# Linear attention on one core: a clear of 128x2080 elements in sixteen instructions, and one load in five DMAs

## Chip, core and metric

The kernel runs on one core of one Trainium2 chip. The metric is the device time of one execution in microseconds (us), taken here as the median of four runs. One further execution was recorded by the hardware profiler, and all rows below come from it.

## What is computed

The inputs Q, K and V have 8 batches, 12 heads, 512 rows and 64 columns, in float32.

```python
Q_feat = np.maximum(0, Q) + 1
K_feat = np.maximum(0, K) + 1
KV = np.einsum('bhkd,bhkv->bhdv', K_feat, V)
K_sum = np.sum(K_feat, axis=2)
numerator = np.einsum('bhqd,bhdv->bhqv', Q_feat, KV)
denominator = np.einsum('bhqd,bhd->bhq', Q_feat, K_sum)
return (numerator / (denominator[:, :, :, None] + 1e-10)).astype(np.float32)
```

For every head a 64x64 matrix KV and a 64-vector K_sum are made from K and V, and each row of Q is multiplied with them and divided. Everything is read once and the result is written once: the page counts 37.75 MB read and 12.58 MB written.

## The kernel before

The 96 heads are worked through in twelve groups of eight heads (g from 0 to 11), and two groups make a pair s. `load("k", ...)` and `load("v", ...)` bring K and V of a group or of a pair into SBUF (the on-chip memory of 128 partitions) and turn float32 into bf16 on the way; `load_q(s)` brings Q of a pair. All these loads are issued by GpSimd (POOL), as are the stores of groups 0 to 9. Only the first K (`load_first_k`) and the last four stores are issued by SyncE (SP).

For each group, `k_features` (VectorE, DVE) makes K_feat; `v_blocks` copies V into a block layout `v_all` in four copies of 32 partitions, of which DVE makes b = 0, 1 and 2 and ScalarE (ACT) makes b = 3 (partitions 96 to 127); `keys_values` (TensorE, PE) accumulates KV and K_sum in `kva_ps`, which ACT casts into the weights `kva_all` (lines 179 and 180). `q_features`, `transposes` and `out_matmuls` make the numerator and denominator, `norms` (DVE) divides, and `store` writes.

`kva_all` holds four slots of four blocks b, each 128 partitions by 130 elements of bf16. Parts of each block must be zero and stay so; the kernel clears them once at its start, on POOL. Slot g % 4 is written by ACT for group g.

The order of instructions on each engine is that of the program text (`manual_schedule`). POOL works in this order: the clear of `zero`, the loads of V of group 0, Q of pair 0, K of group 1, V of group 1; then the identity matrix (`make_identity`, two instructions, needed by the first transposes); then the clear of `kva_all` (line 257); then `load_pair(1)`, which is K, V and Q of pair 1. After that come `load_pair(2)` and the later ones, each K and V load waiting until the compute engines have read the buffer that it overwrites, with two buffers in turn, and the stores.

The loads that POOL issues all go through one software DMA queue, which the page calls q0. In the program as built, DMAs issued by POOL signal their completion on eight semaphores in turn. A DMA that gets a semaphore for the second time is preceded by a wait on POOL until the DMA that used it before, eight DMAs back, has landed; where the same wait has been made already, it isn't made again.

Of the kernel before, what the change touches and what calls it, by code (L numbers as in the profile page):

```python
# [19 lines left out]
def kernel(  # L20
# [19 lines left out]
    nc = tc.nc  # L40

    B, H, S, D = Q.shape
    P = 128
# [36 lines left out]
    kva_all = const.tile([P, NV, 4, 2, D1], BF16, name="kva_all")  # L80
    kva_diag = [kva_all[:, i] for i in range(NV)]

    drams = dict(k=k_dram, v=v_dram)
    raw = {}
    bufs = {}
# [6 lines left out]
    def load_first_k():  # L92
        k_raw = head_pool.tile([P, 2, C2, D], FP32, name="k_first")
        nc.sync.dma_start(out=k_raw, in_=k_dram[:, 0:4:2])
        raw["k", 0] = k_raw

    def load(x, groups):
        s = groups[0] // 2
        if groups[0] % 2 == 0 or (x, s) not in bufs:
            bufs[x, s] = in_pool.tile([P, 4, C2, D], BF16, name=f"{x}_raw")  # L100
        if len(groups) == 2:
            ms = slice(0, 4)
            of = slice(4 * s, 4 * s + 4)
        else:
            ms = slice(groups[0] % 2, 4, 2)
            of = slice(4 * s + groups[0] % 2, 4 * s + 4, 2)
        nc.gpsimd.dma_start(out=bufs[x, s][:, ms], in_=drams[x][:, of])  # L107
        for g in groups:
            raw[x, g] = bufs[x, s][:, g % 2 : 4 : 2]

    def load_q(s):
        t = in_pool.tile([P, 2, C4, D], BF16, name="q_raw")
        nc.gpsimd.dma_start(out=t, in_=q_eights[:, 2 * s : 2 * s + 2])  # L113
        rows = t.rearrange("p n (r c) d -> p n r c d", c=C)
        for e in range(2):
            raw["q", 2 * s + e] = rows[:, :, :, 4 * e : 4 * e + 4]

    def load_pair(s):
        load("k", (2 * s, 2 * s + 1))
        load("v", (2 * s, 2 * s + 1))  # L120
        load_q(s)

    def store(g):
        s = g // 2
        o_to = o_dram[:, 2 * NP * s : 2 * NP * s + 2 * NP]
        if g < NG - 2:
            nc.gpsimd.dma_start(out=o_to[:, g % 2 : 2 * NP : 2], in_=outs[s][:, g % 2 : 2 * NP : 2])  # L127
            return
        for h in range(2):
            nc.sync.dma_start(  # L130
                out=o_to[:, 2 * h + g % 2 : 2 * NP : NP], in_=outs[s][:, 2 * h + g % 2 : 2 * NP : NP]
            )
# [6 lines left out]
    def k_features(g):  # L139
        k_raw = raw.pop(("k", g))  # L140
        kf = kf_pool.tile([P, C2, 2, D], BF16, name="kf")
        for n in range(2):
            feature(kf[:, :, n], k_raw[:, n])
        kfs[g] = kf

    def v_blocks(g):
        v_raw = raw.pop(("v", g))
        for b in range(4):
            ps = slice(32 * b, 32 * b + 32)
            if b == 3:  # L150
                nc.scalar.copy(out=v_blk[g % 2][ps, b], in_=v_raw[ps])  # L151
            else:
                nc.vector.tensor_copy(out=v_blk[g % 2][ps, b], in_=v_raw[ps])  # L153

    def q_features(g):
        q_raw = raw.pop(("q", g))
        qf = qf_pool.tile([P, R, C // 2, 2, D], BF16, name="qf")
        for n in range(2):
            feature(qf[:, :, :, n], q_raw[:, n])
        qfs[g] = qf  # L160

    def keys_values(g):
        kf = kfs.pop(g)
        sb = g % 2
        vb = v_all[:, 4 * sb : 4 * sb + 5]
        kva_ps = psum_kva.tile([P, 5, D], FP32, name="kva_ps")
        for c in range(C2):
            for n in range(2):
                nc.tensor.matmul(  # L169
                    kva_ps[64 * n : 64 * n + 64],  # L170
                    lhsT=kf[:, c, n, :],
                    rhs=vb[:, :, n, c, :],
                    start=(c == 0),
                    stop=(c == C2 - 1),
                )
        kva = kva_diag[g % NV]
        for n in range(2):
            ps = slice(64 * n, 64 * n + 64)
            nc.scalar.copy(out=kva[ps, :, n, 0:D], in_=kva_ps[ps, sb : sb + 4, :])  # L179
            nc.scalar.copy(out=kva[ps, :, n, D], in_=kva_ps[ps, 4 - 4 * sb, 0:4])  # L180

    def transposes(g):
        qf = qfs.pop(g)
        if g % 2 == 0:
            qts[g // 2] = mid_pool.tile([P, C, P, R], BF16, name="qt")
        for half in range(2):
            qt_ps = psum_qt.tile([P, 2, R, P], BF16, name="qt_ps")
            for c in range(2):
                for r in range(R):
                    nc.tensor.transpose(qt_ps[:, c, r], qf[:, r, 2 * half + c, :, :], identity)  # L190
            copy = nc.vector.tensor_copy if half and g == NG - 2 else nc.scalar.copy
            lo = g % 2 * 4 + 2 * half
            copy(out=qts[g // 2][:, lo : lo + 2], in_=qt_ps.rearrange("p c r q -> p c q r"))  # L193

    def out_matmuls(g, h):
        qt = qts[g // 2]
        kva = kva_diag[(g // 2 * 2 + h) % NV]
        ops = [psum.tile([P, 2, BANK], FP32, tag="ps", name="o_ps") for _ in range(2)]
        for c in range(C):
            for j in range(2):  # L200
                b = 2 * (g % 2) + j
                q = 16 * (4 * h + b)
                nc.tensor.matmul(  # L203
                    ops[c // 4][64 * j : 64 * j + 64, c // 2 % 2, (c % 2) * W : (c % 2) * W + W],
                    lhsT=qt[:, c, q : q + 16, :],
                    rhs=kva[:, b],
                    start=True,
                    stop=True,
                )
        cells_of[g, h] = ops  # L210
# [19 lines left out]
    def output(g):  # L230
        for h in range(2):
            out_matmuls(g, h)
            norms(g, h)

    def clear(first, split, end):
        t = v_all.rearrange("p b m c d -> p (b m c d)").bitcast(FP32)
        w = t.shape[1] // 9
        nc.vector.memset(t[:, first * w : split * w], 0.0)  # L238
        nc.scalar.copy(  # L239
            out=t[:, split * w : end * w], in_=zero.to_broadcast([P, (end - split) * w])  # L240
        )

    with tc.manual_schedule():
        nc.gpsimd.memset(zero, 0.0)
        load_first_k()
        load("v", (0,))
        load_q(0)
        load("k", (1,))
        load("v", (1,))
        nc.vector.memset(ones, 0.0)  # L250
        for b in range(4):
            nc.vector.memset(ones[32 * b : 32 * b + 32, b : b + 1], 1.0)  # L252
        clear(0, 3, 5)
        e = v_all[:, 4, :, :, 0:4].rearrange("p n c j -> p (n c) j")
        nc.vector.tensor_copy(out=e, in_=ones[:, None, :].to_broadcast([P, 2 * C2, 4]))
        make_identity(nc, identity)
        nc.gpsimd.memset(kva_all, 0.0)  # L257
        load_pair(1)
        clear(5, 7, 9)
        last = NG - 1  # L260
        for g in range(last - 1):
            if g % 2:
                transposes(g - 1)
            k_features(g)
            v_blocks(g)
            if g >= 2:
                output(g - 2)
            if g % 2:
                transposes(g)
            else:  # L270
                q_features(g)
                q_features(g + 1)
            keys_values(g)
            if g % 2 and g // 2 + 2 < NG // 2:
                load_pair(g // 2 + 2)
            if g >= LAG:
                store(g - LAG)
        k_features(last - 1)
        output(last - 3)
        out_matmuls(last - 2, 0)  # L280
        v_blocks(last - 1)
        k_features(last)
        v_blocks(last)
        keys_values(last - 1)
        store(last - 1 - LAG)
        q_features(last - 1)
        q_features(last)
        keys_values(last)
        norms(last - 2, 0)
        out_matmuls(last - 2, 1)  # L290
        norms(last - 2, 1)
        transposes(last - 1)
        transposes(last)
        output(last - 1)
        output(last)
        for g in range(last - LAG, NG):
            store(g)
# [30 lines left out]
```

## Time and profile before

| | us |
|---|---|
| runs | 126.93, 127.02, 127.17, 126.81 |
| median of the runs | 126.97 |
| the profiled execution's own time | 126.93 |
| its span in the profile | 124.8 |
| DVE, PE, ACT, POOL busy | 89.3, 67.0, 60.5, 25.4 |

The span runs from the first recorded instruction to the last event; 2.13 us of the profiled execution's own time lie outside it. In the lines of a timeline the first number is the start in us from the span's start, the second the busy time, then follow engine, line, operation, the tiles written and read with partitions x elements, and the count; a bracket at the end tells how long the engine had been idle and what ended that. The page's slices are 40 equal parts of the span, 3.12 us each; a digit is a busy share in tenths. For loads that cast, GB/s counts the bf16 bytes that are written, half of the bytes read.

### The profile page before, as it was taken

To read this page: it belongs to the slowest core of one execution; us is meant where nothing else is said; L and a number is where in the kernel's file an instruction comes from. 1 tells how busy PE (TensorE), PEld (TensorE's weight loads), DVE (VectorE), ACT (ScalarE), POOL (GpSimd) and SP (SyncE) were. 2 spreads that over 40 slices of the span, in tenths; PEclk is the share of its full clock that TensorE was granted. 3 is DMA by queue.
4 is the path that set the end of the run, shared out by engine and by line. 5 is a ranking of instruction groups with operands and counts; after the bars stand their busy time and mean duration, and the time that the engine had idled before them with its cause. 6 is when DMAs were issued, how large, how long until landed. Compare 5 with 4: busy or idle time off the path is not lost.

```text
span 124.8 us, 2326 instructions
## 1 busy us (share of the span) xinstructions
PE 67.0 (54%) x960; PEld 51.1 (41%) x960; DVE 89.3 (72%) x189; ACT 60.5 (48%) x86; POOL 25.4 (20%) x37
## 2 busy tenths in 40 slices
PE   0006955300694847729777490069696359965510
PEld 0004634300473736518565380056485246753300
DVE  4893444206999899998899940799958799387940
ACT  7832199306019972776447771600994291373000
POOL 6990023100011540215302150302020200020000
PEclk9999999955589999995999999756999955899855
DMA  3999999999999999999999999999999999999993
GB/s 100 327 219 208 211 195 209 211 213 216 207 212 213 216 214 209 211 213 219 230 410 320 211 211 216 216 341 393 227 211 217 217 263 415 418 415 416 408 394 127
DMA packets 11818, 32.12 MB, mean 257 GB/s; under 512 B 544, under 2 KB 544, under 8 KB 11808
## 3 DMA queue, kind: packets, MB, share of 16 engines
q0 software_dynamic: 10448, 28.84, 97.3%
q1 hardware_dynamic: 1360, 3.15, 6.7%
q8 instruction: 7, 0.11, 0.3%
q14 instruction: 3, 0.02, 0.0%
HBM read 37.75 MB, written 12.58 MB: 403 GB/s over the span
## 4 chain that ended last, share of the span: by engine, by line
DMA 52%; DVE 19%; PE 13%; ACT 7%; issue 3%; POOL 2%; POOLq 0%; DVEq 0%
DMA v_raw<-in_V_dram 52%; PE kva_ps L169 10%; DVE o_sb L221 8%; DVE v_all L153 7%; ACT v_all L151 3%; ACT qt L193 2%; PE qt_ps L190 2%; DVE recip L220 2%; DVE qf L135 1%; DVE qt L193 1%; ACT kva_all L179 1%; PE o_ps L203 1%; POOL v_raw L107 1%; POOL k_raw L107 1%; DVE kf L135 1%
## 5 line engine op out<-in xcount | busy, mean ns | idle before, releaser
L169 PE MATMUL kva_ps<-v_all,kf 128*64 128x320 bf16 x384 | 36.5, 358 | 15.2 <-DVE v_all L153 14.7
L203 PE MATMUL o_ps<-kva_all,qt 128*64 128x130 bf16 x384 | 19.4, 235 | 34.2 <-DVE recip L220 20.3
L169 PEld LDWEIGHTS <-kf 128*64 128x64 bf16 x384 | 26.1, 133 | 23.2 <-DVE v_all L153 15.0
L153 DVE COPY v_all<-v_raw 32x2048 bf16<-32x2048 bf16 x36 | 26.0, 723 | 13.1 <-DMA v_raw<-in_V_dram 12.7
L221 DVE TENSOR_TENSOR o_sb<-o_ps,recip 128x512 f32<-128x512 f32 x48 | 33.2, 692 | 1.7
L151 ACT COPY v_all<-v_raw 32x2048 bf16<-32x2048 bf16 x12 | 22.6, 1893 | 15.3 <-DMA v_raw<-in_V_dram 15.1
L203 PEld LDWEIGHTS <-qt 128*64 128x64 bf16 x384 | 13.5, 115 | 39.4 <-issue 18.9
L179 ACT CAST kva_all<-kva_ps 64x256 bf16<-64x256 f32 x24 | 8.9, 371 | 33.1 <-PE kva_ps L169 33.0
L193 ACT COPY qt<-qt_ps 128x1024 bf16<-128x1024 bf16 x23 | 22.3, 1015 | 3.9 <-PE qt_ps L190 3.5
L127 POOL DMA_DIRECT2D out_dram<-o_sb x10 | 8.5, 855 | 35.3 <-DVE o_sb L221 28.3
L190 PE MATMUL qt_ps<-identity,qf 128*128 128x128 bf16 x192 | 14.0, 228 | 2.5 <-ACT qt L193 2.0
L135 DVE TENSOR_SCALAR kf<-k_raw 128x1024 bf16<-128x1024 bf16 x22 | 8.6, 431 | 7.3 <-DMA k_raw<-in_K_dram 7.3
L190 PEld LDWEIGHTS <-qf 128*128 128x128 bf16 x192 | 11.7, 102 | 5.0 <-issue 3.7
L220 DVE RECIPROCAL recip<-o_ps 128x8 f32<-128x8 f32 x48 | 9.6, 201 | 3.7 <-PE o_ps L203 3.2
L107 POOL DMA_DIRECT2D k_raw<-in_K_dram x6 | 4.8, 801 | 36.0 <-DVE kf L135 36.0
L135 DVE TENSOR_SCALAR qf<-q_raw 128x1024 bf16<-128x1024 bf16 x24 | 8.8, 431 | 2.7 <-DMA q_raw<-in_Q_dram 2.7
L107 POOL DMA_DIRECT2D v_raw<-in_V_dram x7 | 5.4, 766 | 14.5 <-ACT v_all L151 10.7
L238 DVE MEMSET v_all<- 128x3072 f32 (+1 forms) x2 | 4.4, 2192 | 1.1 <-DVE ones L252 0.7
L113 POOL DMA_DIRECT2D q_raw<-in_Q_dram x6 | 4.3, 710 | 0.0
L180 ACT CAST kva_all<-kva_ps 64x4 bf16<-64x4 f32 x24 | 4.1, 169 | 0.0
L239 ACT COPY v_all<-zero 128x2048 f32<-128x2048 f32 x2 | 3.7, 1894 | 0.0
L257 POOL MEMSET kva_all<- 128x2080 bf16 x1 | 1.8, 1825 | 0.0
(13 smaller groups left out, 5.4 us busy)
## 6 DMA issues: line engine op xcount, KB each, us to landing
out_dram<-o_sb POOLq DMA_DIRECT2D x10, 1024.0 KB, 25.6
q_raw<-in_Q_dram POOLq DMA_DIRECT2D x6, 1024.0 KB, 26.4
k_raw<-in_K_dram POOLq DMA_DIRECT2D x5, 1024.0 KB, 21.8
v_raw<-in_V_dram POOLq DMA_DIRECT2D x5, 1024.0 KB, 23.0
out_dram<-o_sb SPq DMA_DIRECT2D x4, 512.0 KB, 4.6
k_first<-in_K_dram SPq DMA_DIRECT2D x1, 1024.0 KB, 4.9
v_raw<-in_V_dram POOLq DMA_DIRECT2D x2, 512.0 KB, 10.6
k_raw<-in_K_dram POOLq DMA_DIRECT2D x1, 512.0 KB, 12.7
```

What stands on the lines that cost most here:

```text
L107: nc.gpsimd.dma_start(out=bufs[x, s][:, ms], in_=drams[x][:, of])
L127: nc.gpsimd.dma_start(out=o_to[:, g % 2 : 2 * NP : 2], in_=outs[s][:, g % 2 : 2 * NP : 2])
L135: nc.vector.tensor_scalar(out=dst, in0=src, scalar1=1.0, scalar2=1.0, op0=ALU.add, op1=ALU.max)
L151: nc.scalar.copy(out=v_blk[g % 2][ps, b], in_=v_raw[ps])
L153: nc.vector.tensor_copy(out=v_blk[g % 2][ps, b], in_=v_raw[ps])
L169: nc.tensor.matmul(kva_ps[64 * n : 64 * n + 64], lhsT=kf[:, c, n, :], rhs=vb[:, :, n, c, :], start=(c == 0), stop=(c == C2 - 1),)
L179: nc.scalar.copy(out=kva[ps, :, n, 0:D], in_=kva_ps[ps, sb : sb + 4, :])
L190: nc.tensor.transpose(qt_ps[:, c, r], qf[:, r, 2 * half + c, :, :], identity)
L193: copy(out=qts[g // 2][:, lo : lo + 2], in_=qt_ps.rearrange("p c r q -> p c q r"))
L203: nc.tensor.matmul(ops[c // 4][64 * j : 64 * j + 64, c // 2 % 2, (c % 2) * W : (c % 2) * W + W], lhsT=qt[:, c, q : q + 16, :], rhs=kva[:, ...
L220: nc.vector.reciprocal(out=recip, in_=cells[:, :, :, :, D:D1])
L221: nc.vector.tensor_tensor(out=o_sb[:, 2 * h + g % 2 : 2 * NP : NP, 4 * i : 4 * i + 4].rearrange("p n (b c) d -> p b c n d", b=2), in0=cell ...
```

## The change

The load of V of group 1 becomes five DMAs, of partitions 0 to 111, 112 to 121, 122 and 123, 124 and 125, and 126 and 127. Together they move the same bytes to the same places. The clear of `kva_all` becomes sixteen instructions, one for each of the four blocks of the four slots, 130 elements on each partition, instead of one of 2080.

```diff
@@ load
-        nc.gpsimd.dma_start(out=bufs[x, s][:, ms], in_=drams[x][:, of])
+        parts = (0, 112, 122, 124, 126, P) if (x, groups) == ("v", (1,)) else (0, P)
+        for lo, hi in zip(parts, parts[1:]):
+            nc.gpsimd.dma_start(out=bufs[x, s][lo:hi, ms], in_=drams[x][lo:hi, of])
@@ start of the schedule
-        nc.gpsimd.memset(kva_all, 0.0)
+        for t in kva_diag:
+            for b in range(4):
+                nc.gpsimd.memset(t[:, b], 0.0)
```

In the program as built, the four further DMAs take four further completion semaphores, so the turn comes round earlier: K of pair 1 now waits on POOL for V of group 0 to land, V of pair 1 for Q of pair 0, Q of pair 1 for K of group 1, and K of pair 2 for the 112-partition part of V of group 1. Before, these four waited for no semaphore of that kind, or, for K of pair 2, for K of group 1. V of pair 2 waits for the other four parts. From Q of pair 2 on, a DMA waits for the same DMAs as before. The b = 0, 1 and 2 copies of V of group 1 wait for the 112-partition part alone, and ACT's copy b = 3 waits for all five parts. The orders of instructions on PE, DVE, ACT and SP are as they were.

## Prediction

> **What bounds the kernel.** I read the slices of the page first, then its table of DMA queues, then the chain of waits.
>
> ```profile
> DMA  3999999999999999999999999999999999999993
> GB/s 100 327 219 208 211 195 209 211 213 216 207 212 213 216 214 209 211 213 219 230 410 320 211 211 216 216 341 393 227 211 217 217 263 415 418 415 416 408 394 127
> q0 software_dynamic: 10448, 28.84, 97.3%
> DMA 52%; DVE 19%; PE 13%; ACT 7%; issue 3%; POOL 2%; POOLq 0%; DVEq 0%
> ```
>
> The sixteen DMA engines are busy in every slice but the first and the last, and one queue, q0, makes up 97.3% of their span. Two rates stand out: about 212 GB/s where casting loads run (bf16 bytes) and about 415 GB/s where stores run. The 36.7 MB that the casting loads read are 18.35 MB written, 86.6 us at 212 GB/s; the 12.58 MB of stores are 30.3 us at 415 GB/s; the first K, 1.05 MB, takes about 3 us. The sum is 120 of the 124.8 us. So the transfers bound the kernel from about 2 us on until the end: a microsecond in which the queue stands dry or an engine of it has more to carry is paid once in full, and a delay elsewhere is free while the queue stays filled. The chain says the same more roughly, with 52% on waits for V. Now the place of the change, on POOL:
>
> ```profile
> 3.56 0.74 POOL L107 DMA_DIRECT2D v_raw<-in_V_dram  x1
> 4.27 0.25 POOL masks.py:197 MEMSET identity<- 128x128 bf16 x1
> 4.60 0.29 POOL masks.py:199 TENSOR_SCALAR_AFFINE_SELECT identity<-identity 128x128 bf16<-128x128 bf16 x1
> 4.83 1.82 POOL L257 MEMSET kva_all<- 128x2080 bf16 x1
> 6.61 1.03 POOL L107 DMA_DIRECT2D k_raw<-in_K_dram  x1
> 7.63 0.80 POOL L107 DMA_DIRECT2D v_raw<-in_V_dram  x1
> 8.42 0.71 POOL L113 DMA_DIRECT2D q_raw<-in_Q_dram  x1
> 16.64 0.77 POOL L107 DMA_DIRECT2D k_raw<-in_K_dram  x1 [7.51 <-DVE kf L135]
> 20.74 0.74 POOL L107 DMA_DIRECT2D v_raw<-in_V_dram  x1 [3.34 <-DVE v_all L153]
> ```
>
> The first line is the load that is split and the fourth the clear that is split; lines five to seven are pair 1, and the last two are K and V of pair 2. POOL stands idle for 7.51 us before K of pair 2. The consumers tell when the transfers land:
>
> ```profile
> 8.20 2.16 DVE L153 COPY v_all<-v_raw 32x2048 bf16<-32x2048 bf16 x3
> 13.04 1.44 DVE L135 TENSOR_SCALAR qf<-q_raw 128x1024 bf16<-128x1024 bf16 x4 [2.69 <-DMA q_raw<-in_Q_dram]
> 15.58 0.76 DVE L135 TENSOR_SCALAR kf<-k_raw 128x1024 bf16<-128x1024 bf16 x2 [1.11 <-DMA k_raw<-in_K_dram]
> 18.11 2.09 DVE L153 COPY v_all<-v_raw 32x2048 bf16<-32x2048 bf16 x3 [1.77 <-DMA v_raw<-in_V_dram]
> 23.39 0.76 DVE L135 TENSOR_SCALAR kf<-k_raw 128x1024 bf16<-128x1024 bf16 x2 [3.19 <-DMA k_raw<-in_K_dram]
> 29.09 2.11 DVE L153 COPY v_all<-v_raw 32x2048 bf16<-32x2048 bf16 x3 [4.93 <-DMA v_raw<-in_V_dram]
> ```
>
> V of group 0, Q of pair 0 (twice the bytes), K of group 1, V of group 1, K and V of pair 1 (twice the bytes) land at 8.2, 13.0, 15.6, 18.1, 23.4 and 29.1 us: in the order of issue, one behind the other, 2.5 us for each MiB read, with no gap. What was issued at 6.61 us lands at 23.4, because the queue is full.
>
> **POOL's time.** Splitting the load adds four DMA issues. An issue occupies POOL for 0.71 to 0.74 us when nothing disturbs it, for 128 partitions of one or two MiB alike, so I take 4 x 0.73 = 2.9 us; for far fewer partitions it could be less, down to 0. The identity then starts at 4.27 + 2.9 = 7.2 us, and is done by 7.8. Its first reader, the transposes of group 0, starts at 14.82 us, so 7 us of cover stay. For the clear I have two rows: 1.82 us for 2080 elements, 0.875 ns each, and 0.25 us for the identity's 128, hence about 0.14 us fixed. Sixteen of 130 elements are 16 x (0.14 + 0.114) = 4.0 us if they don't overlap, and 1.8 us, as before, if their fixed parts overlap entirely. POOL comes to the loads of pair 1 between 9.6 us and 11.8 us, instead of at 6.61; I take 11.8, since single small instructions are what the 0.25 us row shows. The first clear is needed by ACT's cast of `kva_ps` for group 0, at 14.98 us, so 3 us cover all sixteen and more the first four.
>
> **The waits on POOL.** K of pair 1 waits for V of group 0 (8.2 us), already past. V of pair 1 waits for Q of pair 0, and goes at about 13.1 us instead of 7.63. Q of pair 1 waits for K of group 1, and goes at 15.6 us instead of 8.42. Behind these stand only K of pair 2 (16.64 us, now also waiting for the 112 partitions, which land about 17.8 us) and V of pair 2 (20.74 us, already later than its new waits). When must a load be issued so that the queue doesn't run dry? Its predecessor's landing minus the time from issue to data. The latter is bounded by two DMAs: V of group 0 was issued at 1.29 and landed 6.8 us later with 2.5 us of data of its own, so at most 4.3 us; the last stores from SP landed at the least 4.0 us after issue with 1.26 us of data each, so at most 2.7. I take 4.3 us, the dearer and the one from the same queue. K of pair 1 must go by 18.1 - 4.3 = 13.8 us and goes at 11.8, 2 us of cover. V of pair 1 must go by 23.4 - 4.3 = 19.1 and goes at 13.1; Q of pair 1 by 24.8 and goes at 15.6; K of pair 2, behind three more MiB-sized steps, has over 10 us. So all of POOL's delay is hidden, and nothing else gets late next: the cost is 0.
>
> **The consumers of V of group 1.** The DVE copies wait for 112 of 128 partitions, 7/8 of 2.5 us, and may start 0.3 us sooner, while ACT's copy at 18.09 us waits for five semaphores, 4 more at some 0.03 us each (the short "issue" pieces of the chain). Behind ACT's copy stand its copies of `qt` and the next `kva_all` casts, and PE's second `keys_values` waits for it: 0.1 us later at most. The kernel's next need of this is V of pair 2, issued at 20.74 with queue work until 34 us. Nothing reaches the end: 0.
>
> **The queue's own work.** Bytes are unchanged. Each DMA ends with a signal, so there are four more in the queue. One DMA of 2 MiB (13.04 - 8.20 = 4.84 us) costs no more than two of 1 MiB (2.54 and 2.53 us): a DMA's own cost in the filled queue is 5.07 - 4.84 = 0.23 us at most and about nothing at least, where the landings' scatter is as big. For tiny DMAs I take the low part, 0.025 us each: +0.1 us, with bounds of 0 and 0.9.
>
> [...]
>
> The open item is which of the sixteen engines carry the small DMAs. All DMAs of before have 128 partitions, eight to an engine if shared evenly, so one partition is 2.5 / 8 = 0.31 us. The 112 make seven each, and 16 partitions remain. Shared one to an engine, as 10 + 2 + 2 + 2 allows, they cost nothing; begun each time at the same engine, two engines carry 7 + 1 + 3 = 11 partitions, 0.92 us more than before, and six carry seven, 0.31 us less. I take even sharing, which the even load of before is nearest to, and keep both ends.
>
> [...]
>
> **Sum.** 126.93 (the profiled execution's own time) + 0 (POOL) + 0 (consumers) + 0.1 (queue) = 127.03; the median of the runs is 0.04 above that execution, so 127.07, rounded to 127.05.
>
> **Rivals.** The first ends slower: the small DMAs fall on the same engines. As the queue is never dry, the excess on those two is not given back. It decides where the loaded engines are also among the last to finish; it costs 0.92 us then, 127.95, and nothing if they had 0.92 us to spare. For it: nothing in the rows says where a DMA begins. Against it: nothing as well.
>
> The second, also slower: POOL is late. DVE's features and copies run nearly without pause from 6.7 to 10.4 us, and K of pair 1's issue of 1.03 us, against 0.75 elsewhere, shows that POOL suffers beside them. If the clears stood still until 10.4 us, K of pair 1 would go at 14.4, 0.6 us past 13.8: 127.6. Against it: the next two issues, 0.80 and 0.71 us, lie beside the same DVE copies and are not stretched.
>
> The third ends faster: the engines that get one partition less are those that finish last; the end moves by 0.31 us, to 126.65.
>
> **Numbers.** The forecast has 0.45, the first rival 0.22, the second 0.10, the third 0.23. A measurement of this kernel can tell about 0.2%, 0.25 us, from no change. Of the forecast 0.40 lies inside that, the rest above it; a little of the first rival, with engines that have room, lies inside too. Faster 0.23, same 0.42, slower 0.35. The range goes from the third rival, 126.6, to nearly the whole of the first, 127.8.
>
> **What would show it.** Right: POOL's clears end by 12 us, the three loads of pair 1 are issued at about 11.8, 13.1 and 15.6 us, V and K of pair 1 land within 0.2 us of 29.1 and 23.4, the DMA row has 9 in every slice from the second, and V of the last pair is copied at 98.9 us as before. A K of pair 1 that lands more than 0.3 us late with a dip in the DMA row means POOL was late; one that lands late without a dip means that the engines carry unequal loads. A time outside 126.8 to 127.3 makes the forecast wrong.

## The result, and the profile after

The changed kernel took 126.71 us (median of 43 runs, 126.33 to 127.66) against 127.05 us before (64 runs): a ratio of 0.9975, 95% interval [0.9965, 0.9985]. It is faster by 0.34 us, where no change was forecast. The span explains none of it. The profiled execution of the changed kernel has a span of 124.9 us and a time of its own of 126.71 us, the one before had 124.8 and 126.93. What lies outside the span went from 2.13 us to 1.8. So the first thing to compare is not a stage but the end.

The page after, its slices of the DMA engines and three of its four DMA queues (packets, MB, share of the sixteen engines):

```profile
DMA  3999999999999999999999999999999999999992
GB/s 88 332 218 210 210 202 210 210 215 218 204 212 212 213 219 207 212 216 217 232 410 313 211 212 218 216 342 392 229 211 214 220 266 418 422 413 417 400 401 102
q0 software_dynamic: 10608, 28.84, 97.2%
q8 instruction: 7, 0.11, 0.3%
q14 instruction: 5, 0.03, 0.1%
```

The transfers fill the span as they did. The kernel before had `q14 instruction: 3, 0.02, 0.0%`: one packet of 8 KB more now falls inside the span (the fifth packet is of 40 bytes). "Instruction" is the page's name for the kind of this queue, and its 8 KB packets are called code packets below; no row says what they hold. What comes behind the span is seen by asking the DMA view for the stretch from 124.9 to 128.0 us, in 40 slices. First the kernel before, then the changed one:

```profile
GB/s 0 0 0 0 0 0 0 0 0 0 0 0 0 0 0 0 0 106 0 0 0 0 0 0 0 0 0 0 0 0 0 0 0 0 0 0 0 0 0 0
q14 instruction: 1, 0.01, 1.1%
```

```profile
DMA packets 0, 0.00 MB, mean 0 GB/s; under 512 B 0, under 2 KB 0, under 8 KB 0
```

Before, one packet on the instruction queue starts in slice 17 of 0.0775 us, at about 126.27 us, 1.5 us behind the span's end and 0.8 us before the last semaphore event in the trace, at 127.06. After, there is none. The missing packet is found in the changed kernel's span when the DMA view is asked for 75 to 77 us; in the kernel before that stretch holds none:

```profile
q0 software_dynamic: 207, 0.42, 111.9%
q14 instruction: 1, 0.01, 1.0%
```

POOL's timeline after, at the place of the change:

```profile
3.57 2.93 POOL L109 DMA_DIRECT2D v_raw<-in_V_dram  x5
6.45 0.27 POOL masks.py:197 MEMSET identity<- 128x128 bf16 x1
6.80 0.68 POOL masks.py:199 TENSOR_SCALAR_AFFINE_SELECT identity<-identity 128x128 bf16<-128x128 bf16 x1
7.43 4.59 POOL L261 MEMSET kva_all<- 128x130 bf16 x16
11.97 0.78 POOL L109 DMA_DIRECT2D k_raw<-in_K_dram  x1
13.40 0.80 POOL L109 DMA_DIRECT2D v_raw<-in_V_dram  x1 [0.65 <-DMA q_raw<-in_Q_dram]
15.95 0.70 POOL L115 DMA_DIRECT2D q_raw<-in_Q_dram  x1 [1.75 <-DMA k_raw<-in_K_dram]
18.46 0.77 POOL L109 DMA_DIRECT2D k_raw<-in_K_dram  x1 [1.81 <-DMA v_raw<-in_V_dram]
20.97 0.74 POOL L109 DMA_DIRECT2D v_raw<-in_V_dram  x1 [1.74 <-ACT v_all L153]
```

The brackets of V and Q of pair 1 and of K of pair 2 are the new waits, of 0.65, 1.75 and 1.81 us, for Q of pair 0, K of group 1 and V of group 1 to land. In both traces the landings of what POOL issues stand on eight semaphores in turn, numbers 101 to 108, for 29 DMAs before and 33 after.

And the consumers, on DVE's timeline, with ACT's copy of V of group 1 last:

```profile
18.02 2.42 DVE L155 COPY v_all<-v_raw 32x2048 bf16<-32x2048 bf16 x3 [1.56 <-DMA v_raw<-in_V_dram]
23.38 0.76 DVE L137 TENSOR_SCALAR kf<-k_raw 128x1024 bf16<-128x1024 bf16 x2 [2.95 <-DMA k_raw<-in_K_dram]
29.13 2.11 DVE L155 COPY v_all<-v_raw 32x2048 bf16<-32x2048 bf16 x3 [4.99 <-DMA v_raw<-in_V_dram]
98.97 2.14 DVE L155 COPY v_all<-v_raw 32x2048 bf16<-32x2048 bf16 x3 [0.78 <-DMA v_raw<-in_V_dram]
```

```profile
18.76 1.89 ACT L153 COPY v_all<-v_raw 32x2048 bf16<-32x2048 bf16 x1 [0.93 <-DMA v_raw<-in_V_dram]
```

K and V of pair 1 are used at 23.38 and 29.13 us (23.39 and 29.09 before) and V of the last pair at 98.97 (98.91). Everything that the change does to the work is hidden, as forecast; the gain has another source.

### The profile page after: what moved, and what is told of

The parts are those of the page before. It is cut to its first block, busy times and chain, and to the rows that moved or that the text cites. A ratio compares the mean times of both kernels' runs of the same rounds, so it can differ in the third digit from the quotient of the medians.

```text
span 124.9 us, 2354 instructions
## 1 busy us (share of the span) xinstructions
PE 71.5 (57%) x960; PEld 55.2 (44%) x960; DVE 89.5 (72%) x189; ACT 60.5 (48%) x86; POOL 30.4 (24%) x56
## 3 DMA queue, kind: packets, MB, share of 16 engines
q0 software_dynamic: 10608, 28.84, 97.2%
## 4 chain that ended last, share of the span: by engine, by line
DMA 55%; DVE 15%; PE 14%; ACT 8%; issue 2%; POOL 1%; DVEq 0%; ACTq 0%; POOLq 0%
DMA v_raw<-in_V_dram 47%; PE kva_ps L171 12%; DMA q_raw<-in_Q_dram 9%; DVE o_sb L223 7%; DVE v_all L155 5%; ACT qt L195 4%; ACT v_all L153 3%; DVE recip L222 2%; PE o_ps L205 2%; ACT kva_all L181 1%; DVE qt L195 1%; POOL v_raw L109 1%; PE qt_ps L192 0%; ACT kva_all L182 0%; POOL zero L246 0%
## 5 line engine op out<-in xcount | busy, mean ns | idle before, releaser
L171 PE MATMUL kva_ps<-v_all,kf 128*64 128x320 bf16 x384 | 40.5, 385 | 15.6 <-DVE v_all L155 13.2
L171 PEld LDWEIGHTS <-kf 128*64 128x64 bf16 x384 | 29.7, 143 | 23.7 <-DVE v_all L155 15.6
L205 PE MATMUL o_ps<-kva_all,qt 128*64 128x130 bf16 x384 | 20.9, 247 | 28.9 <-DVE recip L222 20.9
L205 PEld LDWEIGHTS <-qt 128*64 128x64 bf16 x384 | 14.8, 122 | 34.4 <-issue 18.2
L192 PE MATMUL qt_ps<-identity,qf 128*128 128x128 bf16 x192 | 13.3, 221 | 2.6 <-ACT qt L195 2.0
L192 PEld LDWEIGHTS <-qf 128*128 128x128 bf16 x192 | 11.1, 99 | 5.1 <-issue 4.1
L109 POOL DMA_DIRECT2D v_raw<-in_V_dram x11 | 7.8, 719 | 17.2 <-ACT v_all L153 16.1
L261 POOL MEMSET kva_all<- 128x130 bf16 x16 | 4.6, 337 | 0.0
```

The lines of the kernel that those rows point to most:

```text
L109: nc.gpsimd.dma_start(out=bufs[x, s][lo:hi, ms], in_=drams[x][lo:hi, of])
L171: nc.tensor.matmul(kva_ps[64 * n : 64 * n + 64], lhsT=kf[:, c, n, :], rhs=vb[:, :, n, c, :], start=(c == 0), stop=(c == C2 - 1),)
L205: nc.tensor.matmul(ops[c // 4][64 * j : 64 * j + 64, c // 2 % 2, (c % 2) * W : (c % 2) * W + W], lhsT=qt[:, c, q : q + 16, :], rhs=kva[:, ...
```

## The experiments

Theory A is the author's guess from the rows above: POOL's code comes in pages, each with a code packet, and the change adds 20 instructions to POOL's stream (87 recorded in the span instead of 67, semaphore instructions included), so a boundary between two pages is passed during the run and no longer in the code behind the last store, where nothing would hide it. "Page" and "boundary" are words of this theory; what the rows have is a packet of 8 KB and the instruction of POOL that it follows. Theories B and C are the two edits themselves: small DMAs that share the engines better, and casts that wait for single blocks. Theory D is any gain of the edits inside the span.

All results in one table. "POOL" is the number of instructions that POOL has more than before; "outside" is the median over the runs of own time minus span, with the kernel before on the same chip in brackets; the spans are medians too, of values given to 0.1 us.

| kernel | POOL | outside, us | span, us | time, us | ratio, 95% interval |
|---|---|---|---|---|---|
| change, first runs | +20 | 1.78 | 124.90 | 126.71 (127.05) | 0.9975 [0.9965, 0.9985] |
| clear alone | +15 | 1.80 (2.13) | 125.30 (125.00) | 127.07 (127.13) | 1.0003 [0.9978, 1.0027] |
| split alone | +5 | 1.78 (2.13) | 125.55 (125.00) | 127.34 (127.13) | 1.0024 [0.9999, 1.0049] |
| 20 idle clears on POOL | +20 | 1.77 (2.13) | 125.25 (125.00) | 127.03 (127.13) | 0.9997 [0.9977, 1.0017] |
| 20 idle copies on ACT | 0 | 2.13 (2.13) | 125.30 (125.00) | 127.42 (127.13) | 1.0012 [0.9990, 1.0034] |
| change again | +20 | 1.80 (2.14) | 125.05 (124.90) | 126.86 (127.05) | 0.9980 [0.9954, 1.0006] |
| 20 idle clears at the end | +20 | 1.76 (2.14) | 125.10 (124.90) | 126.85 (127.05) | 0.9981 [0.9964, 0.9998] |
| 10 idle clears | +10 | 1.77 (2.14) | 125.05 (124.90) | 126.82 (127.05) | 0.9982 [0.9961, 1.0003] |
| clear, load in two parts | +16 | 1.77 (2.14) | 124.90 (124.90) | 126.70 (127.05) | 0.9965 [0.9941, 0.9989] |
| 128 idle clears | +128 | 2.06 (2.15) | 125.10 (125.10) | 127.21 (127.22) | 1.0003 [0.9982, 1.0024] |
| 2 fewer | -2 | 2.03 (2.15) | 125.00 (125.10) | 127.04 (127.22) | 0.9978 [0.9960, 0.9995] |
| 6 fewer | -6 | 2.08 (2.15) | 125.65 (125.10) | 127.73 (127.22) | 1.0047 [1.0023, 1.0071] |
| change and 108 idle clears | +128 | 2.09 (2.13) | 125.05 (125.00) | 127.17 (127.11) | 1.0011 [0.9986, 1.0036] |

Time outside the span is far steadier than the time itself: in the 43 runs and the profiled execution of the change it lay between 1.72 and 1.85 us, in 35 runs of the kernel before on one chip between 2.09 and 2.18. That is why 0.35 us of it can be read where the ratios' intervals are as wide as the effect.

### One part alone

The clear alone:

```diff
-        nc.gpsimd.memset(kva_all, 0.0)
+        for t in kva_diag:
+            for b in range(4):
+                nc.gpsimd.memset(t[:, b], 0.0)
```

> Only the clear in sixteen instructions; the load of V of group 1 is one DMA as before. POOL has 15 instructions more, PE and ACT 3 waits more. Theory A (the gain of 0.3 us is the length of POOL's instruction stream: a code page that was fetched after the last store is fetched within the span instead): own time minus span falls from 2.13 us to about 1.8 if the page boundary lies within these 15 instructions, the row of queue q14 counts 0.03 MB instead of 0.02, the run is 0.3 us faster; if the boundary lies beyond, nothing changes. Theory B (the small DMAs share the sixteen DMA engines better): no change, ratio 1.000, own time minus span 2.13. Theory C (ACT's casts wait for single blocks instead of the whole clear): 0.3 us faster with a shorter span, own time minus span 2.13.

The split alone is the other hunk of the change without this one.

> Only the load of V of group 1 in five DMAs; the clear is one instruction. POOL has 5 instructions more, ACT 2 waits more. Theory A: no change unless the boundary lies within 5 instructions (then own time minus span 1.8 and 0.3 us faster). Theory B: 0.3 us faster, in the span, which falls to 124.5, own time minus span 2.13. Theory C: no change.

Both bring the outside down, to 1.80 and 1.78 us, but their spans are 0.30 and 0.55 us longer than that of the kernel before, and neither gains in sum. For the split the span holds the lost part in plain sight. These are the waits of SP at the end, in the kernel before and then in the split alone (waited for: us in total, times, longest):

```profile
SPq L323 <- PEq L323: 0.7, 2, 0.5
```

```profile
SPq L325 <- PEq L325: 1.0, 2, 0.8
```

SP's wait for PE at the end takes 0.3 us longer. The DMA view of 124.9 to 128.0 us shows the code packet close behind it, in slice 9, at 125.65 us with a span of 125.4:

```profile
GB/s 0 0 0 0 0 0 0 0 0 106 0 0 0 0 0 0 0 0 0 0 0 0 0 0 0 0 0 0 0 0 0 0 0 0 0 0 0 0 0 0
q14 instruction: 1, 0.01, 1.1%
```

So with 5 instructions more the packet comes earlier, still at the end (0.25 us behind the span's end instead of 1.47), and the price, as theory A reads it, is booked inside the span instead of outside. POOL itself can be seen standing still there. These are two rows of its last instructions, first of the kernel before, then of the split alone (count, least/median/greatest duration in ns, first and last start in us):

```profile
L323 POOLq EVENT_SEMAPHORE  x4: 17/17/17, 124.1 to 124.7; - x4
L323 POOLq EVENT_SEMAPHORE_RANGE_CLEAR  x1: 136/136/136, 124.4 to 124.4; - x1
```

```profile
L325 POOLq EVENT_SEMAPHORE  x4: 17/17/17, 124.3 to 125.3; - x4
L325 POOLq EVENT_SEMAPHORE_RANGE_CLEAR  x1: 135/135/135, 125.0 to 125.0; - x1
```

From the first semaphore instruction to that of the second row, the range clear, it is 0.3 us before and 0.7 us in the split alone. In the trace the instruction ahead of the range clear ends 0.03 us before it in the one and 0.40 us before it, at 124.56 us, in the other. The packet starts at 125.65 us, 0.7 us after POOL has gone on: the pause comes first and the packet follows, so it isn't that packet which POOL waits for.

For the kernel before a pause as long lies behind the span, where the trace still holds semaphore events, though it doesn't name the engine that makes them. Semaphore 2 has eighteen of them there in both kernels. From the second to the third it is 0.20 us in the changed kernel and 0.56 us in the kernel before, the other distances agree to 0.01 us, and the last one comes 1.90 and 2.26 us behind the span's end. That pause of 0.36 us is as long as the whole difference outside the span (2.13 against 1.78), and it too is over before the packet starts. By its length, 0.36 against the 0.37 us that POOL stands still longer in the split alone, it is taken here for the same one.

That refutes theory B: the five DMAs alone gain nothing. The clear alone has its packet inside the span (0.03 MB on q14) and nothing behind it, but a span 0.30 us longer, which theory A doesn't explain; neither does C, which wanted a shorter span.

### Only the length

```diff
+    pad = const.tile([P, 1], FP32, name="pad")
...
         load_pair(1)
+        for _ in range(20):
+            nc.gpsimd.memset(pad, 0.0)
         clear(5, 7, 9)
```

> The kernel before with 20 clears of one element per partition of an unused tile added on POOL, after the issue of the loads of pair 1; nothing reads the tile. POOL's stream is as long as with the change, nothing else of the change is in it. Theory A: 0.3 us faster (ratio 0.9975), own time minus span 1.8, queue q14 0.03 MB. Theories B and C: no change, ratio 1.000, own time minus span 2.13.

On ACT instead, with `nc.scalar.copy(out=pad, in_=zero)` at the same place:

> The kernel before with 20 copies of one element per partition added on ACT at the same place, which nothing reads; they end before V of group 0 lands, at least some 0.2 us each. A variant of theory A in which ACT's stream is the one that counts (the change adds 5 instructions there): 0.3 us faster, own time minus span 1.8. Theory A as stated (POOL's stream), B and C: no gain, own time minus span 2.13; the copies may cost up to 0.2 us if they push ACT's first copy of V.

POOL's 20 idle clears take the outside from 2.13 to 1.77 us, ACT's copies leave it at 2.13. Of these two streams it is POOL's that counts. (Queue q14 isn't POOL's alone: with ACT's copies another packet of 8 KB, at 65.5 us before, starts at 48.7 us, and the one behind the span stays.) ACT's copies were dearer than expected, 4.42 us between the two halves of ACT's first clear, which pushed its first copy of V from 8.19 to 10.07 us. The ratio with POOL's clears, 0.9997, was not the 0.9975 expected: the span was 0.25 us longer on this chip, as with the other three kernels of that job.

### The change beside the idle clears, on one chip

> The changed kernel once more, as it is, so that its time and span stand on the same chip and beside the same runs of the kernel before as the other three. Theory A (only POOL's longer instruction stream counts, its price being 0.35 us of the 2.13 us outside the span): own time minus span 1.78 us, span equal to that of 20 clears on POOL within 0.2 us. Rival, theory D (beyond that, the five DMAs or the sixteen clears shorten the span): span 0.3 us below that of the padded kernels, as the first runs seemed to show (124.9 us against 125.0 to 125.5).

The 20 idle clears at the end of the program, behind the last store:

```diff
         for g in range(last - LAG, NG):
             store(g)
+        for _ in range(20):
+            nc.gpsimd.memset(pad, 0.0)
```

> The kernel before with 20 clears of an unused tile on POOL after its last store. POOL's stream is as long as with the change, but the additional code comes last. Theory A: the fetch of the last code page moves from behind the span's end to POOL's last work, from 112 to 120 us; own time minus span 1.78, ratio 0.997 to 0.998. If the page must be fetched before POOL's real work ends to be of use: 2.13 and no change.

Ten instead of 20, after the loads of pair 1:

> The kernel before with 10 instead of 20 clears of an unused tile on POOL, at the place after the loads of pair 1. Theory A: between 5 instructions (page fetched at the end, gain lost in the span) and 15 (fetched within the span) lies the boundary; with 10, queue q14 shows 0.03 MB in the span and own time minus span is 1.78, or else 0.02 MB and the gain is lost. Either way a span as that of before or 0.2 us more.

The change with the load in two DMAs, `parts = (0, 112, P)`:

> The change with V of group 1 in two DMAs of 112 and 16 partitions instead of five; the clear in sixteen. POOL has 16 instructions more than before. Theory A: as the changed kernel, own time minus span 1.78, span within 0.15 us of it. Theory D, in the form that the small DMAs on few engines make the gain: span 0.3 us longer than that of the changed kernel.

All four have 1.76 to 1.80 us outside, spans of 124.90 to 125.10 us, and ratios from 0.9965 to 0.9982 that can't be told from one another. The change gains no more than idle clears that nobody reads (0.9980 against 0.9981), which leaves theory D without support. Behind the loads of pair 1 or at the end, where the 20 clears stand made no difference outside the span (1.77 and 1.76 us). The traces say the same more sharply: in all ten that hold it in POOL's recorded stream, the packet of the boundary starts 0.7 to 3.8 us after POOL's 68th recorded instruction, whatever that instruction is and whether it runs at 23 or at 124 us. The load in two parts is the fastest of the four by its median, 126.70 us, and beats the kernel before by its interval, but not the change beyond the intervals.

### A whole page, and fewer instructions

If a page boundary is what counts, one page more must undo the gain. For a page the author took 128 instructions; no run shows how many bytes an instruction takes, so the number was the author's guess, to be tried by the run. The 128 idle clears are spread:

```diff
         load_pair(1)
+        pads(32)
...
                 load_pair(g // 2 + 2)
+                pads({2: 40, 3: 16, 4: 20, 5: 20}[g // 2 + 2])
```

> The kernel before with 128 clears of an unused tile on POOL, 32, 40, 16, 20 and 20 of them, each time behind the loads of a pair, where POOL waits anyway. [...] Theory A (it is the place of a page boundary in POOL's stream that counts): after one whole page the boundary stands where it stood before, own time minus span is 2.13 again, queue q14 0.03 MB (one whole page more, no other), and the time is that of before or up to 0.3 us more. Rival (any longer stream brings the gain): 1.78 and 0.2 to 0.3 us faster. The clears of the third and fourth pair may delay stores by 1 to 3 us, which the queue hides.

The outside is back at 2.06 us, the ratio at 1.0003, and the code packet behind the span is back as well, in slice 18, at 126.32 us with a span of 124.9:

```profile
GB/s 0 0 0 0 0 0 0 0 0 0 0 0 0 0 0 0 0 0 106 0 0 0 0 0 0 0 0 0 0 0 0 0 0 0 0 0 0 0 0 0
q14 instruction: 1, 0.01, 0.9%
```

(One of its twelve runs, of 200.15 us, has no explanation here and is left out of the medians of outside and span.) What theory A calls a page is thus 128 instructions here, or a whole fraction of that, since no number between 20 and 128 was run. Two fewer than before, and six fewer:

```diff
-        nc.gpsimd.memset(zero, 0.0)
+        nc.vector.memset(zero, 0.0)
-        nc.gpsimd.memset(kva_all, 0.0)
+        nc.vector.memset(kva_all, 0.0)
```

> The kernel before with the clears of zero and of kva_all on DVE instead of POOL, so that POOL's stream is 2 instructions shorter. Theory A: if the boundary now falls behind the last instruction of the execution, the page isn't needed, own time minus span falls to 1.78 without a fetch in the span, 0.35 us faster; if it still falls into the code after the last store, 2.13 as before and ratio 1.000. DVE's start is up to 1 us later, which its 2.7 us wait for Q hides.

For six fewer, the stores of groups 8 and 9 move to SP besides (`if g < NG - 4`):

> As the kernel with 2 fewer on POOL, and the stores of groups 8 and 9 go from SP, in two DMAs each, so that POOL's stream is 6 instructions shorter than before. Theory A as there, with a boundary 4 instructions further back: 1.78 if the page isn't reached, 2.13 if it is. The four DMAs from SP's queue beside POOL's may move the span by some tenths of a us either way.

With two fewer the packet comes later, at 126.95 us, and the outside is 2.03, a small part of the gain; the ratio, 0.9978, is better than this alone would give, by a span 0.1 us shorter. With six fewer the outside stays at 2.08, and no code packet is recorded behind the span, up to the last event at 127.85 us. The semaphore events hold the pause all the same, only later: it is 0.31 us from the fifteenth to the sixteenth of semaphore 2, where the changed kernel has 0.04 (with two fewer, 0.20 instead of 0.04 us from the eleventh to the twelfth). So by theory A the boundary is still reached, the second of the two cases that theory A had for this run, and removing six instructions was not enough to be rid of it. The span of 125.65 us, 0.65 us more than with two fewer, is the cost of moving the two stores.

### The gain taken out of the changed kernel

The change with both its parts, and 108 idle clears behind the loads of pairs 2 to 5, which makes 128 more than before:

```diff
+                pads({2: 48, 3: 20, 4: 20, 5: 20}[g // 2 + 2])
```

> The changed kernel, with both its parts, and 108 clears of an unused tile on POOL besides, 48, 20, 20 and 20 of them behind the loads of pairs 2 to 5. With the change's 20 instructions that is 128 more than before, a whole page. Theory A: the gain goes, own time minus span from 1.78 back to 2.05 to 2.15 us, time as before, ratio 0.999 to 1.003, although the five DMAs and the sixteen clears are all there. Theory D (the parts themselves gain something in the span): ratio stays at 0.9975.

Outside 2.09 us, ratio 1.0011, and the packet behind the span again:

```profile
GB/s 0 0 0 0 0 0 0 0 0 0 0 0 0 0 0 0 0 0 0 0 106 0 0 0 0 0 0 0 0 0 0 0 0 0 0 0 0 0 0 0
q14 instruction: 1, 0.01, 1.0%
```

The five DMAs and the sixteen clears are all in it, and the gain is gone. The pause is back too: 0.51 us from the second to the third event of semaphore 2 behind the span, and 0.50 us with the 128 idle clears, where the changed kernel has 0.20.

## Why the prediction was wrong

The step that failed is the sum. It began with the profiled execution's own time, 126.93 us, and added only what the change does to the work inside the span; the 2.13 us outside were carried over without a thought. They measured 1.78, and the missing 0.35 us, as long as the pause in the events of semaphore 2 (0.56 us before, 0.20 after), is the whole gain. The row that could have warned stood on the page, queue q14 with its code packets, and the DMA view behind the span had the packet at 126.27 us. I didn't ask what a longer stream on POOL does to it.

The rest held. The five issues took 2.93 us together, 2.2 more than the one before (forecast 2.9): 0.55 us for each of the four further ones, less than a full one. The sixteen clears took 4.59 us (forecast 4.0, with 1.8 as the other end), and the second identity instruction stretched from 0.29 to 0.68. POOL came to pair 1 at 11.97 us (forecast 11.8), its V at 13.40 (13.1) and its Q at 15.95 (15.6), all before their need, and the queue never ran dry: the DMA row has a 9 in every slice but the first and the last. That 11.97 is so near to 11.8 is partly luck, since issues cheaper and clears dearer than forecast made up for each other. The rival in which POOL is late had no place: the clears, from 7.43 us until POOL's next issue at 11.97, and DVE's copies of V of group 0, 2.36 us of work from 8.32 us, ran side by side.

The consumers were less right. DVE's copies of V of group 1 began 0.09 us sooner, not 0.3, and ACT's copy 0.67 us later, not 0.1, because the small DMAs land behind the 112 partitions one by one, 0.18 us apart, from 17.93 to 18.66 us. ACT's next cast came at 24.79 us instead of 22.66, but at 23.20 in the second profile of the changed kernel, so most of this isn't the change's. The cover named for it, queue work until 34 us, hid this: V of pair 2 was issued at 20.97 us, after 20.74.

The queue's term of 0.1 us fits the change's span on one chip, 125.05 against 124.90 us, but so do the idle clears that add no DMA (125.05 and 125.10); it isn't shown. What the four further DMAs added to q0 are 160 packets (10608 against 10448) and no bytes (28.84 MB in both). The 0.18 us from landing to landing are seven times the 0.025 us that the prediction took for a small DMA, yet they didn't add up: the next load came no later. The engines' shares, the open item, left no mark: K of pair 1 is used at 23.38 us against 23.39, which even sharing wants, and 16 partitions in one DMA or in four give times that can't be told apart. The third rival named the right sign and nearly the right size, 0.31 us, for a wrong reason: it wanted the span's end to move, and that didn't.

Three things stay open. What POOL does in the pause is not shown; the packet starts only after it. Nor is it shown why there is no such pause inside the run, where the idle clears at the end of the program start every 0.16 us across the 68th recorded instruction without a gap. And why the clear alone, the split alone and the idle clears had spans 0.25 to 0.55 us longer on one chip, and 0.15 to 0.2 at most on another, was not settled; of the split's 0.55, 0.3 is SP's longer wait at the end.

## What to carry to other kernels

A time is the span and what lies around it, and an edit can move the second: compare own time minus span before looking for a cause in a stage, since here it was steady to 0.07 us where the time scattered by 0.3 and more. A gain of a quarter of a per cent from an edit that adds hidden instructions may belong to the number of instructions; idle instructions on the same engine are the test for that, and more of them, here 128, are the counter-test. Such a gain is not a property of the edit, and further lines on that engine may take it away, as the 108 idle clears did here (1.78 to 2.09 us outside).

## What was not expected of the hardware

In the split alone POOL stood still for some 0.37 us at the very end (0.40 us ahead of the range clear, against 0.03 before), and where the events behind the span hold such a pause, as before the change, the time outside was 0.35 us longer (2.13 against 1.78). Whether it came there went by the number of POOL's instructions: 10 to 20 more took the outside to 1.76 to 1.80 us, 128 more brought it back to 2.06 and 2.09, and 2 or 6 fewer left it at 2.03 and 2.08. The code packet comes 0.7 us after the pause and is not its cause (split alone: POOL goes on at 124.96 us, the packet starts at 125.65). During the run POOL's timeline shows no such pause: idle clears across the same place start 0.16 us apart. The four tiny DMAs in the filled queue cost almost no transfer time (K of pair 1 used at 23.38 us against 23.39), but their landings were spread: V of group 1 was complete for ACT 0.74 us after it was ready for DVE (18.76 against 18.02), where the 16 partitions' bytes alone, at 2.5 us for 128, are 0.31 us.
